# A two-layer decoder trunk: where the small loads stand, who sums the second adaLN part, the order ahead of the experts, and 2 MB pieces for units of four

## The chip, the core and the metric

The kernel runs on one core of one Trainium2 chip. The metric is the device time of one execution in microseconds. The engines named below are PE (TensorE matmuls), DVE (VectorE), ACT (ScalarE), POOL (GpSimd) and SP (SyncE, which here does nothing but issue loads). The 16 DMA engines of the core carry every transfer.

## The reference

256 tokens of width 1024 go through two layers. Each layer is conditioned on one vector `c`, whose product with `w_ada` gives six rows of 1024 (shift, scale and gate, once for the token mixing and once for the experts). The weights of the 32 experts of each layer are by far the most of the bytes.

```python
for l in range(DEPTH):                                   # DEPTH = 2
    mod = (silu(c) @ w_ada[l] + b_ada[l])[:, None, :]    # [1024] x [1024, 6144]
    sh1, sc1, gt1, sh2, sc2, gt2 = split(mod, 6)
    h = x * (1 + sc1) + sh1
    q, k, v, u, vs = split(h @ w_in[l], ...)             # five sections of 512 columns
    att = rms_norm(diff_attention(rope(q), rope(k), v, lam)) # 4 heads, 2 maps of 64
    sg  = chunk_spatial_gate(gelu(u), gelu(vs), ...)     # zu * (w_spatial @ LN(zv) + b)
    x = layer_norm(alpha * x + (1 + gt1) * (concat(att, sg) @ w_out[l]))
    h = x * (1 + sc2) + sh2
    ffn = hier_moe(h, ...)      # top 1 of 4 groups, then top 2 of its 8 experts
    x = layer_norm(alpha * x + (1 + gt2) * ffn)          # expert: (silu(h wg) * (h wu)) wd
```

## The kernel before

**One stream of weights.** `add_*` functions write down, in order, every weight piece of both layers (`stream`). A piece is 1 MB, and it goes into one of 18 slots of 1 MB (`RING`). `pump` (L174) issues pieces on SP as long as a slot is free, and `done` (L204), called where the last instruction that reads a piece is written down, gives its slot back. SP works strictly in order, and each load waits for the landing of the load eight before it on the queue. So the transfers run at most 18 pieces ahead of the engines, and a load whose slot is not free holds back all that stand behind it.

**Small loads.** Biases, norms, rotary tables, router weights and the like (`setup_loads`, L326, some thirty loads of 16 bytes to 256 KB) stand in a list `later`; `pump` issues three of them behind each piece, from the first piece on. The last of them are the router weights of both layers, in tiles `rst` of 128 x 384 numbers; POOL copies them into `wrs` (`reorder`, L354). The tile `four` of `scale_rows` (L387), a pattern of ones that PE uses to spread small rows, has the same tag (`aT`) as `rst`, so it takes the buffer of the first `rst`, and DVE writes it in the middle of the rotary step.

**The order of layer 0 up to the experts.** Sections Q, K, VS, U and V of `h @ w_in` on PE, rotary on DVE (`rope`, L679), transposes of q and k (`qk_T`), VS and U with their norm, then `spatial` and four heads of attention (`scores`, `a_T`, `att`). Four PSUM buffers of tag `s` serve the two products `mix` of `spatial` and the first scores; DVE frees the first two with `zu * mix` (L811). Then `wo` (the product with `w_out`, L924), `residual` (L959) and `normalise` (L582).

**Sums of `w_ada`.** The parts `s1` (shift and scale of the mixing), `s2` (those of the experts) and the gates `g1` and `g2` of `w_ada` are 8 MB, 8 MB, 4 MB and 4 MB per layer. `ada_fold` (L485) is a generator of DVE instructions: each multiplies a quarter of a 1 MB piece by a column of silu(c) and adds it to an accumulator that lies in the first piece, four per piece. `fold_on(n)` takes `n` more instructions of part `s2`, `fold_too(n)` of the next layer's `s1`. `ada_sum` (L429) sums the accumulator over the partitions on PE, and multiplies on PE what was not folded. In layer 0 DVE folds pieces 0 to 3 of `s2`; pieces 4 to 7 come behind `w_out`, and PE multiplies them in `routing`.

**Routing and experts.** `routing` (L983) transposes x, forms `h`, the logits, and the places of the tokens. It also splits x into three bf16 parts (`part` on ACT, `subtract` on PE) for the gather on PE. `gate_sum` forms the gate on PE, `gate_copy` copies it out of PSUM. The experts run in 11 units: units 0 to 5 hold two experts with 64 slots each, units 6 to 10 four experts with 32 slots each. For each unit come `gate`, `up` (`proj`, L1265) and `down` (`dps`). Each expert's matrix is 2 MB and is loaded as two pieces of 1 MB, all first halves of a unit ahead of the second halves. Places 0 to 3 hold fixed experts; which expert stands at a later place is read from the sorted choices of the tokens, and an expert that no token chose is passed over by its loads.

Of the kernel before, what the change touches and what calls it, by code (L numbers as in the profile page):

```python
# [27 lines left out]
def kernel(  # L28
# [89 lines left out]

    def down_parts(i):
        if i == NU - 1:  # L120
            return [((0, 4), (0, 512)), ((0, 2), (512, 1024)), ((2, 4), (512, 1024))]
        return [((0, 2), (0, 1024)), ((2, 4), (0, 1024))]

    def add_experts(l):
# [19 lines left out]
    for l in range(L):  # L144
# [22 lines left out]
    slots = [ring.tile([P, 4 * 512], F32, tag=f"w{i}", name=f"w{i}") for i in range(RING)]  # L167
    free = list(range(RING))
    held, slot_of, taken = {}, {}, {}
# [4 lines left out]
    def pump(limit=RING):  # L174
        while pos["issued"] < len(stream) and pos["issued"] - pos["done"] < limit:
            key, src = stream[pos["issued"]]
            slot_of[key] = free.pop(0)
# [13 lines left out]
            v = slots[slot_of[key]]  # L191
# [8 lines left out]
            for d, s_ in later[:3]:  # L200
                nc.sync.dma_start(d, s_)
            del later[:3]

    def done(*keys):  # L204
        for key in keys:
            held.pop(key)
            free.append(slot_of.pop(key))
# [35 lines left out]
    nc.sync.dma_start(badac, b_ada.rearrange("l (s p k) -> p l s k", s=6, k=KD))  # L243
# [374 lines left out]
    def mixing(l, fp, y_prev, sts):  # L618
# [30 lines left out]
        if l > 0:  # L649
# [255 lines left out]
        S.copy(vv[:, 1, :], section(l, V_, 1))  # L905
        ovs = [py.tile([P, 512], F32, tag="s", name=f"att{qc}").rearrange("t (h d) -> t h d", h=H) for qc in range(NTC)]
# [42 lines left out]
        for tci in range(NTC):
            for h in range(2):  # L950
                if tci == 0 and h == 0 and l + 1 < L:
                    asum = ada_sum(l + 1, "s1", 8)
                elif tci == 0 and h == 1 and l + 1 < L:
                    ada_cols(l + 1, 0, asum, fp)
                wo(tci, h, 0)
                residual(tci, h, o_ps[tci][h], gt1, fp)
            normalise(tci)
# [25 lines left out]
    def routing(l, wr, fp):  # L983
# [5 lines left out]
        def part(a, tci):  # L989
# [3 lines left out]
            for h in range(2):  # L993
                k = slice(4 * h, 4 * h + 4)
                S.copy(parts[:, a, tci, k], left[tci][h].rearrange("t (k d) -> t k d", k=4))

        def subtract(a, tci):
            if a == 0:
                left[tci] = [py.tile([P, 512], F32, tag="s", name=f"left{tci}{h}") for h in range(2)]
            for h in range(2):  # L1000
                k = slice(4 * h, 4 * h + 4)
                if a == 0:
                    T.matmul(left[tci][h], ident, X[:, tci, k, :], start=True, stop=False)
                T.matmul(left[tci][h], minus, parts[:, a, tci, k], start=False, stop=True, skip_group_check=(a > 0))
# [19 lines left out]
        if l == 0:  # L1024
            asum2 = ada_sum(l, "s2", KD // 2)
            ada_cols(l, 2, asum2, fp, py)
            gc, bc = affine_cols(l, 1)
            subtract(0, 0)
            make_hT(hk, gc, bc, 0, early)
            part(1, 0)  # L1030
        else:
            gc, bc = affine_cols(l, 1)
# [463 lines left out]
```

## Time and profile before

| what | us |
|---|---|
| median of 3 runs | 1222.11 |
| lowest and highest | 1221.09 and 1224.03 |
| the profiled execution | 1222.26 |
| its span | 1220.4 |
| PE busy, DVE busy, ACT busy | 1064.3, 356.2, 156.8 |

The profiled execution's time is 1.86 us over its span, which is what lies around it. 467.63 MB were moved in the span. The timelines give the start of an instruction from the beginning of the span, its duration, and in brackets how long the engine had been idle and what ended that.

### The profile page before, as it was taken

Reading aid. Unit: us, or ns where it says so; the run is one execution under the profiler, and the core shown is the slowest. Engines: PE = TensorE matmul, PEld = TensorE weight load, DVE = VectorE, ACT = ScalarE, POOL = GpSimd, SP = SyncE. Lnnn points to the kernel's source line nnn. Section 1 sums busy time; section 2 is a strip of 40 time slices with the busy share of each in tenths; the row PEclk is TensorE's granted clock in tenths of the full one; section 3 lists DMA queues with packets and bytes.
Section 4 is the critical chain, followed back from the end, with each engine's and each line's share of the span. In section 5 each row is a group of like instructions: output and inputs, shape, how many; then the busy total and the mean of one; then the engine's idle time right before and its main releaser. Section 6 shows DMA issues by size and latency. Waiting matters only on the chain. (4 is left out here: it accounts for less than half of the span.)

```text
span 1220.4 us, 14341 instructions
## 1 busy us (share of the span) xinstructions
PE 1064.3 (87%) x5353; PEld 425.6 (35%) x5353; DVE 356.2 (29%) x845; ACT 156.8 (13%) x384; POOL 24.2 (2%) x35
## 2 busy tenths in 40 slices
PE   6999998999997886788789998799999878677875
PEld 2465453434342221132135654343434222122221
DVE  1386767211120100030148535721212001003103
ACT  2033132101010100000022323210101000000000
POOL 0200000000000000000000400000000000000000
PEclk8999999999999888999999999999999989889888
DMA  9999988999999999999999954889999999999995
GB/s 320 363 405 368 418 308 357 379 405 421 421 420 421 421 420 422 422 420 420 393 398 398 400 178 140 335 337 404 421 420 421 422 421 422 421 421 421 420 409 193
DMA packets 92494, 467.63 MB, mean 383 GB/s; under 512 B 12445, under 2 KB 12977, under 8 KB 44546
## 3 DMA queue, kind: packets, MB, share of 16 engines
q1 hardware_dynamic: 92050, 465.86, 94.8%
q8 instruction: 45, 0.74, 0.2%
q10 hardware_dynamic: 288, 0.52, 0.1%
q0 software_dynamic: 80, 0.26, 0.1%
q14 instruction: 31, 0.25, 0.1%
HBM read 484.44 MB, written 1.05 MB: 398 GB/s over the span
## 5 line engine op out<-in xcount | busy, mean ns | idle before, releaser
L1270 PE MATMUL up<-w,XT_moe 128*32 128x512 f32 (+1 forms) x1024 | 196.3, 650 | 37.8 <-DMA w<-in_w_up_dram 37.7
L1360 PE MATMUL dps<-w,eaT_moe 128*32 128x512 f32 (+1 forms) x1024 | 196.2, 635 | 37.8 <-DMA w<-in_w_down_dram 29.2
L1270 PE MATMUL gate<-w,XT_moe 128*32 128x512 f32 (+1 forms) x1024 | 192.8, 656 | 27.3 <-DMA w<-in_w_gate_dram 25.1
L1270 PEld LDWEIGHTS up<-w,XT_moe 128*32 128x32 f32 (+1 forms) x1024 | 53.6, 128 | 170.1 <-issue 102.7
L1326 DVE TENSOR_TENSOR act_moe<-sg_moe,up 128x512 f32<-128x512 f32 x22 | 15.1, 687 | 327.5 <-PE up L1270 292.7
L1360 PEld LDWEIGHTS dps<-w,eaT_moe 128*32 128x32 f32 (+1 forms) x1024 | 52.7, 126 | 165.3 <-issue 98.1
L1270 PEld LDWEIGHTS gate<-w,XT_moe 128*32 128x32 f32 (+1 forms) x1024 | 53.1, 129 | 160.1 <-issue 108.0
L624 PE MATMUL sec<-w,hT_front 128*128 128x512 f32 x192 | 86.5, 605 | 2.6 <-DMA w<-in_w_in_dram 2.4
L1366 DVE TENSOR_TENSOR eo_moe<-dps,gt 128x512 f32<-128x512 f32 x44 | 30.4, 691 | 199.9 <-PE dps L1360 199.9
L1279 PE MATMUL y<-eo_moe,wt_moe 128*128 128x512 f32 x176 | 84.9, 607 | 1.6 <-DVE eo_moe L1366 1.6
L1249 PE MATMUL gps<-G_moe,Xp_moe 128*128 128x256 bf16 (+1 forms) x672 | 64.5, 250 | 3.7 <-DVE G_moe L1223 1.5
L1255 DVE TENSOR_SCALAR XT_moe<-gps,gc,bc 128x128 f32<-128x128 f32 x88 | 30.6, 404 | 123.8 <-PE gps L1249 123.8
L1316 ACT ACTIVATE sg_moe<-gate 128x512 f32<-128x512 f32 x22 | 13.1, 597 | 416.4 <-PE gate L1270 416.4
L1249 PEld LDWEIGHTS <-Xp_moe 128*128 128x128 bf16 x672 | 53.2, 98 | 21.9 <-issue 12.9
L624 PEld LDWEIGHTS sec<-w,hT_front 128*128 128x128 f32 x192 | 36.1, 193 | 45.7 <-issue 41.2
L494 DVE SCALAR_TENSOR_TENSOR w<-w,csl,w 128x512 f32<-128x512 f32 x68 | 47.3, 760 | 0.0
L1279 PEld LDWEIGHTS y<-eo_moe,wt_moe 128*128 128x128 f32 x176 | 30.2, 191 | 43.7 <-issue 40.3
L1294 ACT COPY wt_moe<-wtps 128x256 f32<-128x256 f32 x22 | 8.2, 372 | 286.8 <-PE wtps L1292 286.8
L1258 ACT ACTIVATE XT_moe<-gps,bc,gc 128x128 f32<-128x128 f32 x88 | 33.7, 456 | 41.2 <-PE gps L1249 41.2
L633 PE MATMUL sec<-w,hT_front 128*128 128x512 f32 x64 | 30.1, 625 | 1.9 <-DVE hT_front L647 1.9
L816 PE MATMUL u<-hT_front,w 128*128 128x256 f32 x128 | 28.8, 379 | 0.0
L929 PE MATMUL wo<-w,zu_front 128*128 128x512 f32 x64 | 28.1, 592 | 0.0
(282 smaller groups left out, 745.1 us busy)
## 6 DMA issues: line engine op xcount, KB each, us to landing
w<-in_w_gate_dram SPq DMA_DIRECT2D x128, 1024.0 KB, 17.3
w<-in_w_up_dram SPq DMA_DIRECT2D x128, 1024.0 KB, 17.5
w<-in_w_down_dram SPq DMA_DIRECT2D x120, 1024.0 KB, 16.0
w<-in_w_ada_dram SPq DMA_DIRECT2D x40, 1024.0 KB, 15.4
w<-in_w_in_dram SPq DMA_DIRECT2D x20, 1024.0 KB, 14.9
w<-in_w_ada_dram SPq DMA_DIRECT2D x16, 512.0 KB, 6.1
w<-in_w_out_dram SPq DMA_DIRECT2D x8, 1024.0 KB
w<-in_w_down_dram SPq DMA_DIRECT2D x16, 512.0 KB, 11.3
```

Of the source, the lines that this page charges most:

```text
L494: yield V.scalar_tensor_tensor(acc[:, c], w[:, c], csl[:, k:k + 1], acc[:, c], op0=ALU.mult, op1=ALU.add)
L624: T.matmul(ps, hT[:, k, tci * P:(tci + 1) * P], held["in", l, s, k // 4][:, k % 4, :], start=(k == 0), stop=(k == KD - 1))
L633: T.matmul(ps, hT[:, k, tci * P:(tci + 1) * P], held["in", 0, s, hf][:, k % 4, :], start=(k == 0), stop=(k == KD - 1))
L816: T.matmul(ps[:, 0:NT], held["in", l, U_, k // 4][:, k % 4, g * P:(g + 1) * P], hT[:, k, :], start=(k == 0), stop=(k == KD - 1))
L929: T.matmul(o_ps[tci][h], (cat, zu)[hf][:, kk, tci * P:(tci + 1) * P], w[:, kk, :], start=(hf == 1 and kk == 0), stop=(hf == 0 and kk == 3))
L1249: T.matmul(ps[:, k - kk].rearrange("p j s -> p (j s)"), parts[:, a, tci, k, :], g[:, tci, js[0] * P:(js[-1] + 1) * P], start=(a == 0 and t ...
L1255: V.tensor_scalar(dst, ps[:, k - kk, i, :], gc[:, k:k + 1], bc[:, k:k + 1], op0=ALU.mult, op1=ALU.add)
L1258: S.activation(dst, ps[:, k - kk, i, :], AF.Identity, scale=gc[:, k:k + 1], bias=bc[:, k:k + 1])
L1270: T.matmul(ps[c0:c0 + w], xt[:, k, c0:c0 + w], held[nm, l, place, k // 4][:, k % 4, :], start=(k == 0), stop=(k == KD - 1))
L1279: T.matmul(y[tci][h], wt[:, tci, :], eo[:, h, :], start=(i == 0), stop=(i == NU - 1))
L1360: T.matmul(dps[h][s0:s0 + w], aT[:, kk, s0:s0 + w], held["down", l, place, part][:, kk - ks[0], c0:c0 + 512], start=(kk == 0), stop=(kk == ...
L1366: V.tensor_tensor(eo[:, h, :], dps[h], gt2[:, h * 512:(h + 1) * 512], op=ALU.mult)
```

## The change

It has five parts.

1. **Small loads.** `pump` issues none of `later` behind the first eleven pieces; from the twelfth on three behind each. `badac` joins the list. The copies by POOL are written down after the first columns of the mixing.
2. **Part `s2` of layer 0.** Pieces 4 to 7 stand ahead of `w_out` in the stream, and `ada_fold` runs over all eight. `fold_on(12)`, which stood there without effect in layer 0, now takes pieces 4 to 6; piece 7 follows after section V. `ada_sum` and `ada_cols` move into `wo` in both layers.
3. **Routing.** Both layers take one order: the affine columns and the first half of `h` ahead of `normalise(1)`, first casts of both halves ahead of the second ones, and `gate_copy` directly behind the last cast. `left` of the second half lies in another pool.
4. **Layer 1's head.** Section Q is loaded ahead of the second half of `g1`, and the second half of `gate_sum` follows section Q.
5. **Units 6 to 9.** An expert's matrix is one load of 2 MB into two neighbouring slots (`choose`); all other pieces stay at 1 MB.

```diff
+    def in_parts(i):
+        return [(0, 8)] if (FIXED + WIDE) // 2 <= i < NU - 1 else [(0, 4), (4, 8)]
...
         if l > 0:
-            add_ada(l, "g1", range(4))
-            add_in(l, [Q_, K_, VS_])
+            add_ada(l, "g1", range(2))
+            add_in(l, [Q_])
+            add_ada(l, "g1", range(2, 4))
+            add_in(l, [K_, VS_])
...
             add_ada(l + 1, "s1", range(4, 8))
+            add_ada(l, "s2", range(4, 8))
         add_out(l)
-        if l == 0:
-            add_ada(l, "s2", range(4, 8))
...
+    both = [ring.tile([P, 8 * 512], F32, tag=f"w{i}", name=f"w{i}") for i in range(RING // 2)]
+    slots = [both[i // 2][:, i % 2 * 2048:i % 2 * 2048 + 2048] for i in range(RING)]
...
+    def choose(whole):
+        pairs = [i for i in free if i ^ 1 in free]
+        if whole:
+            return [min(pairs[0], pairs[0] ^ 1), max(pairs[0], pairs[0] ^ 1)] if pairs else None
+        if last and last[0] ^ 1 in free:
+            return [last[0] ^ 1]
+        return (pairs or free)[:1] or None
...
-            for d, s_ in later[:3]:
-                nc.sync.dma_start(d, s_)
-            del later[:3]
+            if pos["issued"] >= 12:
+                for d, s_ in later[:3]:
+                    nc.sync.dma_start(d, s_)
+                del later[:3]
...
-        for k in range(4 if (l, part) == (0, "s2") else KD):
+        for k in range(KD):
...
         S.copy(vv[:, 1, :], section(l, V_, 1))
+        if l == 0:
+            fold_on(6)
...
         part(0, 0)
-        if l == 0:
-            asum2 = ada_sum(l, "s2", KD // 2)
-            ada_cols(l, 2, asum2, fp, py)
...
+        gc, bc = affine_cols(l, 1)
+        make_hT(hk, gc, bc, 0, early, both=False)
+        gsum = gate_sum(l, "g2", 5)
+        subtract(0, 0)
+        normalise(1)
...
+        gate_sum(l, "g2", 5, gsum)
         subtract(1, 1)
         part(2, 1)
+        gr = gate_copy(l, 5, gsum, fp)
...
+            assert not later
+            for f in copies:
+                f()
```

**SP, start of layer 0, before.** The router weights (`rst0`, `rst1`) and their neighbours on the queue. `w10` to `w13` hold sections K and VS of `w_in`, `w14` to `w17` pieces 0 to 3 of `s2`, `w0` and `w1` section U.

```order
L201 DMA lncol_144<-in_ln2_b_dram 128x2x8
L201 DMA rst0_front0_179<-in_w_group_dram 128x32
L201 DMA rst0_front0_179<-in_w_router_dram 128x4x64
L197 DMA w12_90<-in_w_in_dram 128x4x512
L201 DMA rst1_front0_180<-in_w_group_dram 128x32
L201 DMA rst1_front0_180<-in_w_router_dram 128x4x64
L197 DMA w13_91<-in_w_in_dram 128x4x512
L197 DMA w14_92<-in_w_ada_dram 128x2048
```

**SP, the same loads after.** `w8` holds pieces 2 and 3 of `s2`, `w0` section U, each as two halves of a pair.

```order
L224 DMA w8_86<-in_w_ada_dram 128x2048
L229 DMA wsp0_front0_168<-in_w_spatial_dram 128x4x128
L229 DMA lncol_134<-in_ln1_g_dram 128x2x8
L229 DMA lncol_134<-in_ln1_b_dram 128x2x8
L224 DMA w0_78<-in_w_in_dram 128x4x512
L229 DMA lncol_134<-in_ln2_g_dram 128x2x8
L229 DMA lncol_134<-in_ln2_b_dram 128x2x8
L229 DMA rst0_front0_169<-in_w_group_dram 128x32
L224 DMA w0_78<-in_w_in_dram 128x4x512
L229 DMA rst0_front0_169<-in_w_router_dram 128x4x64
```

The router weights stood ahead of section VS and all of `s2`; now they stand behind these and behind section U.

**SP, after, later in layer 0.** Each row is a load, `x4` four in a row: the piece of `s1` that goes into the first half of `w8`, and pieces 4, 5 and 6 of `s2`, which all go into its second half; then piece 7 into `w0`, and `w_out`.

```order
L224 DMA w7_85<-in_w_ada_dram 128x2048
L224 DMA w8_86<-in_w_ada_dram 128x2048 x4
L224 DMA w0_78<-in_w_ada_dram 128x2048
L224 DMA w0_78<-in_w_out_dram 128x4x512
L224 DMA w1_79<-in_w_out_dram 128x4x512
```

Before, pieces 4 to 7 had four slots of their own, behind `w_out`; here three pieces share one half, one after the other.

**DVE, layer 0, before, from the norm of `zv` to the softmax.** `sgps` are the norm's scale and shift, `w2` the first piece of the next layer's `s1`, `lam` the attention's lambda, `zu<-zu,mix` the end of `spatial`, `mx` the first maximum over `scores`.

```order
L722 TENSOR_SCALAR zv_front0_361<-zv_front0_361,sgmv_488,sgrs_513 128x128 x8
L727 TENSOR_TENSOR zv_front0_361<-zv_front0_361,sgps_571 128x512 x2
L727 TENSOR_TENSOR zv_front0_361<-zv_front0_361,sgps_575 128x512 x2
L492 TENSOR_SCALAR w2_80<-w2_80,csl_171 128x512 x4
L385 COPY lam_170<-lamps_607 128x2
L811 TENSOR_TENSOR zu_front0_524<-zu_front0_524,mix_610 128x4x128
```

**DVE, the same place after.**

```order
L751 TENSOR_SCALAR zv_front0_352<-zv_front0_352,sgmv_479,sgrs_504 128x128 x8
L756 TENSOR_TENSOR zv_front0_352<-zv_front0_352,sgps_562 128x512 x2
L756 TENSOR_TENSOR zv_front0_352<-zv_front0_352,sgps_566 128x512 x2
L522 SCALAR_TENSOR_TENSOR w7_85<-w8_86,csl_161,w7_85 128x512 x12
L520 TENSOR_SCALAR w1_79<-w1_79,csl_161 128x512 x4
L413 COPY lam_160<-lamps_612 128x2
L840 TENSOR_TENSOR zu_front0_515<-zu_front0_515,mix_615 128x4x128
```

Twelve instructions have come in between, the sums of the pieces 4, 5 and 6 that SP's list above puts into one half slot.

**ACT, routing of layer 1, before.** `rsy` is the root of `normalise(1)`, `Xp` the bf16 parts, `hT` the transposed input of the router.

```order
L558 ACTIVATE rsy_4603<-rsv_4601 128x1
L559 ACTIVATE rsy_4603<-rsy_4603 128x1
L991 CAST Xp_moe1_4615<-X_98 128x8x128
L615 ACTIVATE hT0_moe1_4616<-hTps_4619,bc1_1_4631,gc1_1_4630 128x128 x4
L615 ACTIVATE hT1_moe1_4617<-hTps_4624,bc1_1_4631,gc1_1_4630 128x128 x4
L995 CAST Xp_moe1_4615<-left00_4644 128x4x128
```

**ACT, the same place after.**

```order
L1025 CAST Xp_moe1_4542<-X_89 128x8x128
L643 ACTIVATE hT0_moe1_4543<-hTps_4546,bc1_1_4558,gc1_1_4557 128x128 x4
L643 ACTIVATE hT1_moe1_4544<-hTps_4551,bc1_1_4558,gc1_1_4557 128x128 x4
L586 ACTIVATE rsy_4598<-rsv_4596 128x1
L587 ACTIVATE rsy_4598<-rsy_4598 128x1
L643 ACTIVATE hT1_moe1_4544<-hTps_4611,bc1_1_4558,gc1_1_4557 128x128 x4
```

The first cast and the first half of `hT` have moved ahead of the root of `normalise(1)`.

## Rows read from the trace of the kernel before

**Rows 1.** The page: transfer rate in 40 slices of 30.5 us each.

```profile
GB/s 320 363 405 368 418 308 357 379 405 421 421 420 421 421 420 422 422 420 420 393 398 398 400 178 140 335 337 404 421 420 421 422 421 422 421 421 421 420 409 193
```

**Rows 2.** Stretches: busy PE, PEld, DVE, ACT, POOL, clock, DMA share, GB/s.

```profile
210.00:220.00 10.00, 10.00 (x42) 3.39 (x41) 3.82 (x5) 0.00 (x0) 0.00 (x0) 0.86 0.52 198
...
720.00:750.00 30.00, 26.36 (x82) 12.41 (x78) 15.56 (x35) 2.99 (x8) 0.00 (x0) 0.98 0.52 175
840.00:1140.00 300.00, 257.31 (x1370) 88.05 (x1366) 42.89 (x80) 17.92 (x44) 0.00 (x0) 0.93 1.01 421
```

**Rows 3.** Timeline of PE, layer 0: start, duration, instruction, [idle before, releaser].

```profile
156.90 1.04 PE L603 MATMUL hTps<-ident,X 128*128 128x128 f32 x8
157.87 1.06 PE L433 MATMUL ada_s<-w,onec 128*32 128x512 f32 x8
158.75 3.62 PE L438 MATMUL ada_s<-w,csl 128*32 128x512 f32 x32
163.07 1.09 PE L478 MATMUL adaT<-ident,adar_moe 128*64 128x128 f32 x8 [0.71 <-ACT adar_moe L473]
...
185.41 4.94 PE L1270 MATMUL gate<-w,XT_moe 128*64 128x512 f32 x22 [0.76 <-ACT gr_moe L520]
```

**Rows 4.** Timeline of DVE, layer 0.

```profile
56.12 0.64 DVE L391 COPY four_front<-ident 16x128 f32<-16x128 f32 x1
56.89 0.69 DVE L685 TENSOR_TENSOR ropea_front<-sec,cos 128x512 f32<-128x512 f32 x1
...
60.76 0.69 DVE L685 TENSOR_TENSOR ropea_front<-sec,cos 128x512 f32<-128x512 f32 x1 [1.85 <-PE sec L633]
...
62.37 0.41 DVE L690 TENSOR_TENSOR ropea_front<-ropea_front,ropeb_front 128x256 f32<-128x256 f32 x1
...
73.10 5.39 DVE L494 SCALAR_TENSOR_TENSOR w<-w,csl,w 128x512 f32<-128x512 f32 x8
...
93.22 0.16 DVE L385 COPY lam<-lamps 128x2 f32<-128x2 f32 x1 [0.67 <-PE lamps L384]
94.50 0.69 DVE L811 TENSOR_TENSOR zu_front<-zu_front,mix 128x512 f32<-128x512 f32 x1 [1.12 <-PE mix L808]
```

**Rows 5.** Timelines of SP and POOL, layer 0: router weights loaded, and copied.

```profile
40.62 0.60 SPq L201 DMA_DIRECT2D rst_front<-in_w_router_dram  x1
...
46.27 0.40 POOL L356 COPY wr<-rst_front 128x256 f32<-128x256 f32 x1
```

**Rows 6.** Stretches, columns as above: the start, and one of 2 KB rows.

```profile
0.00:60.00 60.00, 47.42 (x164) 20.16 (x165) 14.33 (x40) 10.03 (x15) 10.36 (x25) 0.94 0.99 341
60.00:70.00 10.00, 9.76 (x29) 4.51 (x28) 9.08 (x18) 2.36 (x3) 0.00 (x0) 1.00 1.03 400
...
660.00:670.00 10.00, 10.00 (x34) 5.84 (x33) 8.46 (x25) 3.09 (x5) 0.00 (x0) 1.00 1.05 385
```

**Rows 7.** DMA issues: count, KB of one, median us from issue to landing.

```profile
out_dram<-o_moe ACTq DMA_DIRECT2D x2, 256.0 KB, 2.2
```

**Rows 8.** Timelines of PE, DVE and ACT, routing of layer 1.

```profile
742.75 1.04 PE L603 MATMUL hTps<-ident,X 128*128 128x128 f32 x8
...
748.19 0.39 PE L1004 MATMUL left<-Xp_moe,minus 128*128 128x512 bf16 x1 [3.54 <-ACT Xp_moe L991]
...
768.53 3.65 PE L1270 MATMUL gate<-w,XT_moe 128*64 128x512 f32 x16 [1.37 <-ACT gr_moe L520]
...
745.01 1.28 DVE L586 BATCH_NORM_STATS2 bnst<-X 128x6 f32<-128x512 f32 x2
...
748.60 0.17 DVE L546 TENSOR_SCALAR gc<-modc 128x8 f32<-128x8 f32 x1
...
749.34 2.90 ACT L615 ACTIVATE hT_moe<-hTps,bc,gc 128x128 f32<-128x128 f32 x8 [1.21 <-DVE gc L550]
```

**Rows 9.** Timeline of PE, start of layer 1.

```profile
621.06 8.80 PE L624 MATMUL sec<-w,hT_front 128*128 128x512 f32 x16 [2.39 <-DMA w<-in_w_in_dram]
...
630.90 7.10 PE L624 MATMUL sec<-w,hT_front 128*128 128x512 f32 x16 [0.16 <-DVE hT_front L613]
```

More of the change, by code (lines that the diff above doesn't have):

```diff
@@ L176, in pump @@
             key, src = stream[pos["issued"]]
-            slot_of[key] = free.pop(0)
+            whole = key[0] in ("gate", "up", "down") and key[3] in ((0, 8), ((0, 4), (0, 1024)))
+            got = choose(whole)
+            if got is None:
+                break
+            for i in got:
+                free.remove(i)
+            slot_of[key] = got
+            last[:] = got[-1:]
             cond = {}
@@ L190, in pump @@
                 src = src(taken[l, place][1] if place >= FIXED else None)
-            v = slots[slot_of[key]]
+            v = both[got[0] // 2] if whole else slots[got[0]]
             if len(src.shape) == 4:
@@ L206, in done @@
             held.pop(key)
-            free.append(slot_of.pop(key))
+            free.extend(slot_of.pop(key))
             pos["done"] += 1
@@ L954, in mixing @@
                     ada_cols(l + 1, 0, asum, fp)
+                elif tci == 1 and h == 0:
+                    asum2 = ada_sum(l, "s2", KD)
+                elif tci == 1 and h == 1:
+                    ada_cols(l, 2, asum2, fp)
                 wo(tci, h, 0)
                 residual(tci, h, o_ps[tci][h], gt1, fp)
-            normalise(tci)
+                if tci == 0 and h == 0:
+                    fold_on(4)
+            if tci == 0:
+                normalise(0)
     def residual(tci, h, ps, gt, pool):
@@ L1156, in routing @@
         hTs.clear()
-        return gc, bc, Xp, posm, rest, places, gsum
+        return gc, bc, Xp, posm, rest, places, gr
     def spill(l, gc, bc, Xp, ovc, ci, gt, mp):
@@ L1210, in last_rows, with experts @@
         return fg, fb
-    def experts(l, gc, bc, Xp, posm, rest, places, gsum, mp):
+    def experts(l, gc, bc, Xp, posm, rest, places, gr, mp):
         Gs, Ws, XTs = {}, {}, {}
@@ L1268, in proj @@
             for k in range(KD):
+                part = next(q for q in in_parts(i) if q[0] <= k < q[1])
                 for place, c0, w in UNITS[i]:
                     T.matmul(ps[c0:c0 + w], xt[:, k, c0:c0 + w],
-                             held[nm, l, place, k // 4][:, k % 4, :], start=(k == 0), stop=(k == KD - 1))
-                if k % 4 == 3:
-                    done(*[(nm, l, place, k // 4) for place, _, _ in UNITS[i]])
+                             held[nm, l, place, part][:, k - part[0], :], start=(k == 0), stop=(k == KD - 1))
+                if k == part[1] - 1:
+                    done(*[(nm, l, place, part) for place, _, _ in UNITS[i]])
             return ps
@@ L1396 @@
             pump()
-            for f in copies:
-                f()
             def x_in():
@@ L1427 @@
         mp = moe_pool(l)
-        gc, bc, Xp, posm, rest, places, gsum = routing(l, wrs[l], mp)
-        y, sts, fin = experts(l, gc, bc, Xp, posm, rest, places, gsum, mp)
+        gc, bc, Xp, posm, rest, places, gr = routing(l, wrs[l], mp)
+        y, sts, fin = experts(l, gc, bc, Xp, posm, rest, places, gr, mp)
         if l + 1 == L:
```

64 lines of the change are left out of this document (24 added, 40 removed).

## The prediction

> **What bounds the kernel now.** I read the rates over the span first, then single stretches, and then the order of the instructions where the transfers stop. For most of the span the DMA engines move 420 to 422 GB/s [rows 1], and in units of four experts they are busy all the time while PE is not: 257.31 of 300 us, DMA share 1.01 [rows 2]. There only the transfers count. But the rate falls in two places, ahead of the experts of each layer: 198 at 210 us, 175 between 720 and 750 us [rows 2]. PE is busy there nearly without a gap. The ring of 18 pieces is full and nothing is loaded until an engine gives a slot back. So a microsecond on the chain PE, DVE, ACT ahead of the experts is a microsecond of the total, in either layer, and a lost stretch of transfers is never made up behind it, since the transfers are at their rate there. That is the frame of the sum: layer 0's chain, layer 1's chain, and the rate in units 6 to 9.
>
> **Small loads (layer 0).** They go from places behind the first pieces to places behind the twelfth and later ones. The last are the router weights. In the trace SP issues those of layer 0 by 41.2 us and POOL has copied them at 46.67 us [rows 5], well ahead of their reader. But `four` lies in the same buffer as the first `rst`, so DVE must wait with it for POOL's copy; it ran at 56.12 us without any wait [rows 4]. After the change 21 pieces' worth of weights and x, 22.0 million bytes, and some 0.7 million of small loads (by their shapes) are ahead of `rst`. The stretch to 60 us moved 341 GB/s, thus 20.5 million bytes, the next one goes at 400 [rows 6]; the remaining 2.2 million take 5.6 us, and the load lands near 66.5. Copies of 0.6 us and `four` of 0.64 follow, so the rotation of k starts near 68.0 in place of 56.89. Behind `four` on DVE stand both rotations of k, all folds, and the norm of `zv`; on PE, the transposes of k and behind them sections VS and U. The two rotations ended at 62.8 after 5.9 us, of which 1.85 were a wait for PE that is now over [rows 4]; they end at 68.0 + 4.0 = 72.0. **A = +9.2 us.** Bounds: were everything ahead moved at 421 from the start, `rst` would land near 58 and A be about +1; if the wait inside stays, +11. I take the value from the row whose bytes are the same.
>
> **Pieces 4 to 6 of `s2` (layer 0).** They pass, one after the other, through one half slot: SP may issue piece 5 only when DVE has folded piece 4, and piece 6 only when it has folded piece 5. Piece 4 is long there, since it waits only for the fold of piece 3. The twelve folds stand on DVE ahead of `lam` and of `zu * mix`. One fold takes 5.39 / 8 = 0.674 us [rows 4], twelve take 8.1. Between them lie two loads of 1 MB on a queue that SP's wait has emptied. A store of 256 KB lands 2.2 us after its issue [rows 7]; 0.62 of that is its transfer at 421 GB/s, so 1.6 is fixed, and 1 MB takes 2.5 + 1.6 = 4.1. Two are 8.2. Two waits of DVE for PE, 0.67 and 1.12 [rows 4], disappear. **B = 8.1 + 8.2 - 1.8 = +14.5 us**, between 12 (a shorter latency) and 18 (transfers still queued ahead). Nothing covers it: the second pair of scores needs the PSUM buffers that `zu * mix` frees, PE stands there with section V behind them, and SP itself holds back piece 7, `w_out` and the experts. Piece 7's four folds, 2.7 us, come after section V, where DVE has waits; nothing is added for them.
>
> PE stands idle for about ten microseconds in each of the two waits. After a wait of 2.39 us its sixteen matmuls of a section took 8.80 us, the same sixteen without a wait 7.10 [rows 9]: **+1.7**, counted once; 0 to 3.4.
>
> **Routing of layer 0.** From the end of `wo` at 156.90 to the first expert matmul at 185.41 are 28.5 us [rows 3]. `ada_sum` takes 1.06 + 3.62 there and `adaT` 0.71 + 1.09. The multiplications of 3.62 go altogether; the rest, 1.06 and 1.09, goes into `wo`, where PE is busy, and costs 2.1 there. With layer 1's new order (next) 21.5 remain. **-28.5 + 21.5 + 2.1 = -4.9 us**; -2 to -7.
>
> **Routing of layer 1.** From 742.75 to 768.53 are 25.8 us [rows 8]. The first half of `hT` on ACT waits for `gc`, which DVE writes behind `normalise(1)`: 748.60 [rows 8]. Without `normalise(1)`, which begins at 745.01 [rows 8], `gc` is made there, and `hT` starts 4 us sooner; PE's wait of 3.54 us goes. Then `normalise(1)` is late: its 3.6 us of DVE now stand behind, and the second half of `h` comes only 3 us sooner. The gate's copy, for which PE waited 1.37 us, now stands ahead of the gather. Together -3.0 - 1.2 = -4.2. At the head Q's load saves the 2.39 us of its wait, but part of the gate's sum comes behind Q: -1.3 of a possible -2.4 [rows 9]. **-5.5 us**; -3 to -7.
>
> **2 MB pieces.** Units 6 to 9 of both layers are 201 million bytes, 478 us at 421. An SBUF row of a piece becomes 16 KB in place of 8. In a stretch of 2 KB rows (`w_in`) the rate is 385 [rows 6], of 8 KB rows 421. 16 x 8192 bytes take 340 and 311 ns, so each of three more starts of a row costs 9.7 ns. One start less per 16 KB gives 613 in place of 622.6 ns, 428 GB/s, and 7.5 us on the whole. **-6 us**, as experts without tokens are passed over; 0 to -7.5, zero if the rows are cut at 8 KB. A unit waits longer for its first matmul, since a pair must be there whole, but five of the nine pairs, 25 us of transfers, are queued behind the four in use, and a pass over them takes 7 us.
>
> **Sum.** 9.2 + 14.5 + 1.7 - 4.9 - 5.5 - 6 = +9.0 on 1222.26, the profiled execution's own time (span 1220.4 and 1.86 around it; 0.15 above the median): **1231 us**.
>
> **Rivals.** *The router weights land early* (A near +1, no idle PE there): 1223. For it: small loads are what slows the start, and the first 13 MB lose them. Against: they only move, ahead of `rst` still. *The transfers, not the engines, end layer 0's front*, the case on the other side: then A, B and the gain of that routing are all absorbed, and -5.5 - 6 gives 1211. It decides if DMA's share ahead of the experts stays near 1. For it: 363 to 418 GB/s in slices two to five, up to 152 us [rows 1]. Against: 0.52 at 210 us [rows 2], where PE is fully busy. *The 2 MB pieces bring nothing*, because rows are cut or a pair is waited for: 1237. The Trainium skill, "DMA: Bandwidth & Descriptors", "Rules for kernel authors", asks for 1 MiB or more per DMA for the full bandwidth; every piece has that already, so by that rule the sum is 1237 too. *PE falls back to 1.2 GHz between its bursts in units of four* and becomes their bound: 257 us at a clock of 0.93 would be 479 for 300 [rows 2], far over 1300. The Trainium skill, "TensorE: Matmul & The Clock Gate", "HAM oscillation", tells of kernels that wait for DMA between matmuls and lose the clock so. Against: at 0.93 the units' present waits already cost almost nothing.
>
> **Chances.** Forecast 0.54, early router weights 0.13, absorbed 0.14, nothing from 2 MB 0.17, clock 0.02. The range 1216 to 1242 holds the forecast with its bounds, the first and the third rival; the absorbed case, the clock and the ends of the bounds stay out. About 0.2% is what a measurement of this kernel can tell from no change. Below 1219.7 lie the absorbed case and a tail of the first: 0.18. Within 0.2%: 0.10. Above: 0.72.
>
> **What would show it.** A: `four` near 67 us behind POOL. B: DVE waiting twice for a load of `w_ada`, about 4 us each, ahead of `zu * mix` near 118 to 120, and PE idle there. Layer 1: first expert matmul 21 to 22 us behind the end of `wo`. 2 MB: near 428 GB/s in units of four. It is wrong if DVE does not stand at those two loads, or if the first experts of layer 0 start before 195 us (forecast: near 206).

## The result: slower by 2.7%, and where the time went

| | us |
|---|---|
| before, median of 4 runs beside the changed kernel | 1223.07 |
| changed, median of 4 runs | 1257.66 (1254.87 to 1259.13) |
| ratio, 95% interval | 1.0269 (1.0239 to 1.0298) |
| the profiled execution and its span | 1259.13, 1257.5 |
| forecast | 1231 (1216 to 1242) |

The sign was right, the size was not: +34.6 us in place of +9.0. The same events, read from both traces (their spans lie 37.1 us apart, the medians 34.6), show where the distance between the two kernels grows:

| event | before | changed | shift | forecast |
|---|---|---|---|---|
| layer 0: second rotation of k ends | 62.78 | 77.47 | +14.7 | +9.2 |
| `zu * mix` starts | 94.50 | 130.62 | +36.1 | +23.7 |
| end of `wo` (first `hTps`) | 156.90 | 197.06 | +40.2 | +27.5 |
| first expert matmul | 185.41 | 223.74 | +38.3 | +20.5 |
| layer 1: second Q section | 630.90 | 670.32 | +39.4 | +16.2 |
| end of `wo` | 742.75 | 782.11 | +39.4 | +16.2 |
| first expert matmul | 768.53 | 810.47 | +41.9 | +12.0 |
| end of the span | 1220.4 | 1257.5 | +37.1 | +9.0 |

Nearly all of it is lost in layer 0 before `zu * mix`. The page of the changed kernel says the same in its rate over 40 slices (answers [rows 1]) and in the granted clock of TensorE below it: slices four and five, 94 to 157 us, fall from 368 and 418 to 265 and 149 GB/s, and the clock digits of slices three to five read 7, 8 and 8.

```profile
GB/s 347 303 382 265 149 409 280 330 378 410 420 425 341 428 429 426 429 428 376 416 392 405 395 362 160 163 343 404 422 421 426 430 426 429 427 428 428 420 412 211
PEclk8978898999999788778999999799999988788998
```

**Layer 0's front.** DVE's timeline in the changed kernel (answers [rows 4]; start, duration, instruction, [idle before, releaser]): `four` waits 16.44 us for POOL, which itself waits for a load of the router weights (first row, from POOL's timeline), and each fold of pieces 4, 5 and 6 waits for its load.

```profile
72.09 0.40 POOL L384 COPY wr<-rst_front 128x256 f32<-128x256 f32 x1 [2.55 <-DMA rst_front<-in_w_router_dram]
...
72.52 0.21 DVE L419 COPY four_front<-ident 16x128 f32<-16x128 f32 x1 [16.44 <-POOL wr L384]
...
110.92 2.74 DVE L522 SCALAR_TENSOR_TENSOR w<-w,csl,w 128x512 f32<-128x512 f32 x4 [3.34 <-DMA w<-in_w_ada_dram]
118.62 2.74 DVE L522 SCALAR_TENSOR_TENSOR w<-w,csl,w 128x512 f32<-128x512 f32 x4 [4.96 <-DMA w<-in_w_ada_dram]
126.31 2.74 DVE L522 SCALAR_TENSOR_TENSOR w<-w,csl,w 128x512 f32<-128x512 f32 x4 [4.95 <-DMA w<-in_w_ada_dram]
...
130.62 1.28 DVE L840 TENSOR_TENSOR zu_front<-zu_front,mix 128x512 f32<-128x512 f32 x2
```

PE follows, with one wait for each of the two, and computes at the low clock behind both: section VS, 16 matmuls, takes 9.11 us, the next section 7.03, and the first scores behind the second wait 1.39 in place of 0.49.

```profile
74.86 1.09 PE L726 MATMUL qkTps<-ident,ropea_front 128*128 128x128 f32 x4 [13.74 <-DVE ropea_front L719]
79.58 9.11 PE L652 MATMUL sec<-w,hT_front 128*128 128x512 f32 x16
...
88.96 7.03 PE L652 MATMUL sec<-w,hT_front 128*128 128x512 f32 x16
...
113.24 0.49 PE L767 MATMUL s<-qk_front 64*128 64x128 f32 x4
...
131.36 1.39 PE L767 MATMUL s<-qk_front 64*128 64x128 f32 x4 [16.56 <-DVE zu_front L840]
```

Stretches of the changed kernel (columns as in [rows 2]) show what that leaves of the transfers. From 60 to 107 us the queue never empties. Then pieces 5 and 6 go through the half slot one after the other, each issued when the fold ahead of it has ended (at 113.69 and 121.39 us), and the second piece of `w_out` waits for one more fold (issued at 139.42). These stretches run at 27 to 289 GB/s, and the granted clock of PE falls to 0.50, which is 1.2 GHz.

```profile
0.00:60.00 60.00, 47.79 (x164) 20.31 (x165) 11.70 (x34) 10.05 (x15) 2.63 (x18) 0.91 0.93 327
60.00:107.00 47.00, 33.26 (x104) 19.42 (x103) 30.47 (x77) 11.12 (x16) 7.59 (x7) 0.82 1.02 387
...
110.00:120.00 10.00, 4.64 (x35) 3.51 (x34) 4.12 (x7) 1.67 (x2) 0.00 (x0) 0.89 0.30 106
120.00:130.00 10.00, 0.00 (x0) 0.00 (x0) 5.05 (x10) 0.00 (x0) 0.00 (x0) 0.50 0.76 289
130.00:140.00 10.00, 8.64 (x21) 4.38 (x22) 8.76 (x26) 3.44 (x16) 0.00 (x0) 0.59 0.07 27
```

**The routing.** From the end of `wo` to the first expert matmul are 26.7 us in layer 0 (28.5 before) and 28.4 in layer 1 (25.8 before, [rows 8]). The timeline of layer 1's routing, ACT, DVE and PE: the eight copies of `hT(0)` stand on ACT ahead of `rsy` of `normalise(1)`, DVE waits 2.19 us for it and PE 2.47 for the normalised X. Behind that wait both products of the logits take 3.61 us.

```profile
785.24 2.89 ACT L643 ACTIVATE hT_moe<-hTps,bc,gc 128x128 f32<-128x128 f32 x8
...
787.99 0.23 ACT L586 ACTIVATE rsy<-rsv 128x1 f32<-128x1 f32 x1
...
788.49 0.22 DVE L592 SCALAR_TENSOR_TENSOR rst<-rsy,rsv 128x1 f32<-128x1 f32 x1 [2.19 <-ACT rsy L587]
...
790.00 1.88 PE L631 MATMUL hTps<-ident,X 128*128 128x128 f32 x8 [2.47 <-DVE X L616]
...
791.74 3.61 PE L1053 MATMUL rt<-wr,hT_moe 128*128 128x36 f32 x16
...
795.22 3.61 PE L1053 MATMUL rt<-wr,hT_moe 128*128 128x36 f32 x16
```

**Units of four.** Two stretches of the kernel before, in the units of four of either layer; then three of the changed kernel: the end of layer 0's units of two, and the units of four of either layer. 428 and 426 GB/s stand where 421 stood, as forecast; but in layer 0 the queue is empty for 3.4 us just ahead of them.

```profile
370.00:560.00 190.00, 148.08 (x854) 44.40 (x847) 25.51 (x46) 7.90 (x19) 0.00 (x0) 0.90 1.01 421
985.00:1160.00 175.00, 137.16 (x738) 41.31 (x742) 22.89 (x38) 8.70 (x20) 0.00 (x0) 0.87 1.01 421
...
380.00:390.00 10.00, 10.00 (x48) 4.01 (x47) 1.98 (x5) 1.50 (x4) 0.00 (x0) 1.00 0.44 161
390.00:560.00 170.00, 122.55 (x671) 35.40 (x673) 14.23 (x28) 6.29 (x15) 0.00 (x0) 0.81 1.01 428
1030.00:1200.00 170.00, 124.16 (x726) 39.52 (x726) 22.18 (x37) 8.16 (x20) 0.00 (x0) 0.84 1.01 426
```

### The profile page after: what moved, and what is told of

Its sections match the earlier page's. It is cut to its first block, busy times and chain, and to the rows that moved or that the text cites. A ratio compares the mean times of both kernels' runs of the same rounds, so it can differ in the third digit from the quotient of the medians.

```text
span 1257.5 us, 13892 instructions
## 1 busy us (share of the span) xinstructions
PE 1057.6 (84%) x5319; PEld 431.9 (34%) x5321; DVE 366.9 (29%) x857; ACT 158.2 (13%) x388; POOL 24.1 (2%) x35
## 5 line engine op out<-in xcount | busy, mean ns | idle before, releaser
L1296 PE MATMUL up<-w,XT_moe 128*32 128x512 f32 (+1 forms) x1024 | 188.6, 651 | 42.0 <-DMA w<-in_w_up_dram 42.0
L1296 PE MATMUL gate<-w,XT_moe 128*32 128x512 f32 (+1 forms) x1024 | 184.1, 650 | 31.7 <-DMA w<-in_w_gate_dram 31.7
L522 DVE SCALAR_TENSOR_TENSOR w<-w,csl,w 128x512 f32<-128x512 f32 x72 | 50.0, 762 | 13.3 <-DMA w<-in_w_ada_dram 13.2
L1305 PEld LDWEIGHTS y<-eo_moe,wt_moe 128*128 128x128 f32 x176 | 30.2, 191 | 43.6 <-issue 40.2
L960 PE MATMUL wo<-w,cg_front 128*128 128x512 f32 x64 | 28.9, 597 | 0.0
```

The lines of the kernel that those rows point to most:

```text
L522: yield V.scalar_tensor_tensor(acc[:, c], w[:, c], csl[:, k:k + 1], acc[:, c], op0=ALU.mult, op1=ALU.add)
L960: T.matmul(o_ps[tci][h], (cat, zu)[hf][:, kk, tci * P:(tci + 1) * P], w[:, kk, :], start=(hf == 1 and kk == 0), stop=(hf == 0 and kk == 3))
L1296: T.matmul(ps[c0:c0 + w], xt[:, k, c0:c0 + w], held[nm, l, place, part][:, k - part[0], :], start=(k == 0), stop=(k == KD - 1))
L1305: T.matmul(y[tci][h], wt[:, tci, :], eo[:, h, :], start=(i == 0), stop=(i == NU - 1))
```

## The experiments

Ratios are to runs of the kernel before on the same chip; comparisons across the table go by them. 0.1% is 1.2 us.

| kernel | median us | ratio (95%) |
|---|---|---|
| changed | 1257.66 | 1.0269 (1.0239 to 1.0298) |
| `e1_four_alone` | 1256.41 | 1.0281 (1.0261 to 1.0300) |
| `e2_pe_half` | 1236.76 | 1.0123 (1.0102 to 1.0143) |
| `e3_both` = e1 + e2 | 1220.93 | 0.9973 (0.9955 to 0.9991) |
| `e4_one_mb` | 1254.80 | 1.0279 (1.0254 to 1.0304) |
| `e5_old_routing` = e3, routing as before | 1217.97 | 0.9966 (0.9954 to 0.9978) |
| `e6_norm_first` = e3, `normalise(1)` first | 1208.36 | 0.9884 (0.9865 to 0.9903) |
| `e7_before_2mb` | 1218.63 | 0.9976 (0.9966 to 0.9986) |
| `e8_before_head` | 1219.64 | 0.9977 (0.9967 to 0.9986) |
| `e9_norm_only` | 1243.66 | 1.0166 (1.0138 to 1.0194) |
| `e10_pieces_early` | 1212.49 | 0.9916 (0.9893 to 0.9938) |
| `e11_old_loads` = e6, small loads as before | 1205.78 | 0.9863 (0.9840 to 0.9887) |
| `e12_one_mb` = e6, 1 MB | 1214.41 | 0.9927 (0.9907 to 0.9948) |

### Layer 0's front: one wait behind another

**`e1_four_alone`** takes away what made `four` wait.

```diff
-    def scale_rows(fp):
+    def scale_rows(zv):
...
-        four = fp.tile([NROW, 4, 32], F32, tag="aT", name="four")
+        four = zv[0:NROW, 1, 0:P].rearrange("r (a b) -> r a b", a=4)
...
-            scale_rows(fp)
+            scale_rows(zv)
```

> The changed kernel with one edit: `four` is written into the part of `zv` that is still unused, no longer into the buffer that the router weights' `rst` held. The router weights arrive as late as before the edit. Theory: the late buffer holds DVE up by 14 to 17 us, so `four` runs near 58 us in place of 72.5 (when the last row of `rw` has landed), the second rotation of k ends near 64, `zu * mix` starts near 116 in place of 130.6, and the time is 1241 to 1244. Rival (the transfers end layer 0's front, so what DVE gains is waited for later): `four` runs early too, but the end of `wo` stays near 197 and the time near 1257.

The rival was right. `four` ran at 56.09 us, the second rotation ended at 63.25, and nothing was gained: 1.0281 beside 1.0269. DVE's timeline in this kernel, and two stretches of it, say why: it reached piece 4 at 93.3 us, 14 us sooner than in the changed kernel, and then stood 16.59 us there. The fold of piece 4 starts near 110 in both, although SP had issued its load by 90.2 us here and by 97.8 in the changed kernel: what was queued ahead of the load set its arrival, not the time at which the half slot came free. PE did nothing from 100 to 120.

```profile
56.09 0.21 DVE L419 COPY zv_front<-ident 16x128 f32<-16x128 f32 x1
...
109.90 2.74 DVE L522 SCALAR_TENSOR_TENSOR w<-w,csl,w 128x512 f32<-128x512 f32 x4 [16.59 <-DMA w<-in_w_ada_dram]
...
100.00:110.00 10.00, 0.00 (x0) 0.00 (x0) 0.10 (x1) 0.00 (x0) 0.00 (x0) 0.56 0.69 289
110.00:120.00 10.00, 0.00 (x0) 0.00 (x0) 4.84 (x8) 0.00 (x0) 0.00 (x0) 0.50 0.30 105
```

**`e2_pe_half`** leaves the lock on `four` and gives pieces 4 to 7 back to PE; **`e3_both`** has both edits.

```diff
+        add_out(l)
+        if l == 0:
             add_ada(l, "s2", range(4, 8))
-        add_out(l)
...
     def ada_fold(l, part):
         acc = held["ada", l, part, 0][:, 0, :]
-        for k in range(KD):
+        for k in range(4 if (l, part) == (0, "s2") else KD):
...
-                    asum2 = ada_sum(l, "s2", KD)
+                    asum2 = ada_sum(l, "s2", KD if l else KD // 2)
```

> The changed kernel with one edit: pieces 4 to 7 of layer 0's `s2` are loaded behind `w_out` and multiplied by PE in `ada_sum` (which stays where the change put it, in `wo`), not folded by DVE. Theory: the three waits of DVE of 3.3, 5.0 and 5.0 us and the folds between them go, `zu * mix` starts 19 us sooner (near 111.5); PE multiplies 3.6 us more in `wo`; the time is 1240 to 1243. If only the folds cost and the waits move elsewhere: 1249. If transfers end the front: 1257.

> Both edits, `four` in `zv` and pieces 4 to 7 multiplied by PE. Theory: the two losses lie one behind the other on DVE and add, so 1257.7 - 15 - 16 = 1227 (1224 to 1230). Rival: both hide the same wait (the transfers of the front), so the second edit brings less than 8 us beside the first and the time is 1234 or more.

`e2_pe_half` started `zu * mix` at 110.72 and came out at 1236.76, some 18 to 21 us below the changed kernel, a little more than expected. `e3_both` started it at 96.58 (94.50 before) and came out at 1220.93, lower than expected. In both (first `e2_pe_half`, then `e3_both`) DVE waits there for PE as before, and for no load:

```profile
110.72 0.69 DVE L841 TENSOR_TENSOR zu_front<-zu_front,mix 128x512 f32<-128x512 f32 x1 [1.12 <-PE mix L838]
...
96.58 0.69 DVE L841 TENSOR_TENSOR zu_front<-zu_front,mix 128x512 f32<-128x512 f32 x1 [1.12 <-PE mix L838]
```

On the same chip the lock on `four` is thus worth 1236.76 - 1220.93 = 15.8 us where the pieces are out of the way and nothing where they are not; the pieces are worth 1256.41 - 1220.93 = 35.5 us where `four` is out of the way. The two losses do not add, because the second is a wait until a fixed time (the arrival of piece 4) and swallows the first.

**`e10_pieces_early`** asks what makes piece 4 late: the bytes queued ahead of it, or the one half slot. DVE folds all eight pieces, as in the change, but they stand eight places sooner in the stream (with `four` in `zv` and `normalise(1)` first, as in `e6_norm_first` below).

```diff
         if l + 1 < L:
+            add_ada(l, "s2", range(4, 8))
             add_ada(l, "g1", range(4))
             add_ada(l + 1, "s1", range(4, 8))
-            add_ada(l, "s2", range(4, 8))
         add_out(l)
```

> `four` in `zv`, `normalise(1)` ahead of `hT(0)`, and DVE folds all eight pieces of layer 0's `s2` as in the change; but pieces 4 to 7 are loaded ahead of `g1` and of the second four of layer 1's `s1`, eight places sooner in the stream. Theory (the long wait is for bytes that are queued ahead of piece 4): it lands near 88 us, before DVE comes to it, the folds run without waiting, `zu * mix` comes 8 us later than with PE's multiplications (near 104 instead of 95.7), `wo` is 3.6 us shorter: 1211 to 1214. Rival (the half slot through which the pieces pass is the cause, whatever their place): DVE still waits about 5 us twice and the time is above 1220.

1212.49, as the theory had it. DVE's timeline: the twelve folds run as one block of 8.02 us behind the norm of `zv`, without any wait, and `zu * mix` follows at 103.00.

```profile
91.01 2.46 DVE L756 TENSOR_TENSOR zv_front<-zv_front,sgps 128x512 f32<-128x512 f32 x4
93.40 8.02 DVE L522 SCALAR_TENSOR_TENSOR w<-w,csl,w 128x512 f32<-128x512 f32 x12
101.35 1.65 DVE L520 TENSOR_SCALAR w<-w,csl 128x512 f32<-128x512 f32 x4
103.00 1.26 DVE L840 TENSOR_TENSOR zu_front<-zu_front,mix 128x512 f32<-128x512 f32 x2
```

So the place in the stream was the fault, not the folding by DVE. At the new place each piece also has a slot of its own, or the folds could not run without a load between them; so this run takes the bytes ahead of piece 4 and the shared half slot away together. That the bytes made piece 4 late is seen in `e1_four_alone`; the waits of 5 us for pieces 5 and 6 are the half slot's. The folding may still cost more than PE's multiplications do (0.9916 beside 0.9884 of `e6_norm_first`, with intervals that just overlap; in the traces the first expert starts at 189.85 and 183.71 us).

### The routing: one item of ACT's queue

**`e5_old_routing`** puts the routing of before back into `e3_both`; **`e6_norm_first`** keeps the new order there and moves one call; **`e9_norm_only`** moves that call in the changed kernel and leaves all else.

```diff
         part(0, 0)
         gc, bc = affine_cols(l, 1)
+        normalise(1)
         make_hT(hk, gc, bc, 0, early, both=False)
         gsum = gate_sum(l, "g2", 5)
         subtract(0, 0)
-        normalise(1)
```

> The kernel with both edits (`four` in `zv`, pieces 4 to 7 multiplied by PE) and, beside them, the routing in the order of before for both layers: `normalise(1)` back in `mixing`, the second `hTps` on the other PSUM pool, the gate's copy behind the first gather; `ada_sum` stays in `wo`. The prediction held that the new order saves 4.2 us in layer 1 and about 0.5 in layer 0, so going back would cost: 1225 to 1226. The theory from the traces (the new order makes PE wait 2.5 us for `X` ahead of the second `hTps` and compute the logits at 1.2 GHz; routing 26.7 us in either layer against 25.8 in layer 1 before and 28.5 - 6.5 = 22.0 in layer 0): going back saves 0.8 + 4.7, so 1215 to 1216.

> The kernel with both edits and one more: in the routing, `normalise(1)` stands ahead of the copies of `hT(0)`, so that ACT makes `rsy` before those eight copies. Theory: DVE's 2.2 us wait for `rsy` and PE's 2.5 us wait for `X` go, in both layers: -4.4, and up to 1.5 us a layer more if PE then keeps 2.4 GHz through the logits: 1213 to 1217. Rival (the logits are what ends the routing, at 1.2 GHz whatever stands ahead): the routing keeps 26.7 us, 1220 to 1222.

> The changed kernel with one edit alone: `normalise(1)` ahead of the copies of `hT(0)` in the routing. The two losses of layer 0's front stay. Theory (each routing falls to 20.0 us at a full clock, as with both other edits): 26.7 to 20 in layer 0 and 28.4 to 20 in layer 1, so -15 and 1241 to 1244. Rival (in the run with both other edits something else of the front brought part of it): 1250.

`e5_old_routing` does not differ from `e3_both` (0.9966 and 0.9973). The new order as it was written brought nothing; but the second expectation overstated it too, since without `ada_sum` the old order took 26.8 us in layer 0, not 22.0. Moving `ada_sum` into `wo`, with PE multiplying pieces 4 to 7, put 5.8 us there (1.06 + 3.62 + 1.09 by [rows 3]) and took only 1.7 out of that routing (28.5 to 26.8); no run makes this move alone.

`e6_norm_first` gained 0.89%, about 11 us, more than either expectation. The same stretch, end of `wo` to the first expert, takes 20.0 us in both layers. Rows of the two routings in `e3_both` (first two) and in `e6_norm_first` (last two):

```profile
164.49:191.18 26.69, 23.30 (x155) 15.18 (x153) 12.20 (x45) 12.18 (x28) 0.00 (x0) 0.81 0.67 268
745.00:771.68 26.68, 23.28 (x155) 15.37 (x153) 12.21 (x45) 12.19 (x28) 0.00 (x0) 0.81 0.47 178
...
163.67:183.71 20.04, 18.34 (x155) 11.59 (x153) 12.21 (x45) 12.16 (x28) 0.00 (x0) 1.00 0.89 359
737.20:757.25 20.05, 18.33 (x154) 11.57 (x152) 12.22 (x45) 12.16 (x28) 0.00 (x0) 1.00 0.65 236
```

DVE and ACT do the same 12.2 us of work; PE's busy time falls from 23.3 to 18.3, since the granted clock is 1.00 and not 0.81. The timeline of layer 1 in `e6_norm_first` shows the cause: `rsy` stands ahead of the copies, PE waits 0.79 us in place of 2.47, and each product of the logits takes 1.95 us in place of 3.61.

```profile
741.43 0.20 ACT L587 ACTIVATE rsy<-rsv 128x1 f32<-128x1 f32 x1 [1.00 <-DVE rsv L585]
...
743.41 1.09 PE L632 MATMUL hTps<-ident,X 128*128 128x128 f32 x8 [0.79 <-DVE X L617]
...
744.37 1.95 PE L1054 MATMUL rt<-wr,hT_moe 128*128 128x36 f32 x16
...
746.18 1.95 PE L1054 MATMUL rt<-wr,hT_moe 128*128 128x36 f32 x16
```

Of the 6.65 us of a routing, some 1.7 are the shorter wait; 5 are the clock. `e9_norm_only` gained 1.0% (14 us between the medians) with both routings at 20.04 us and a clock of 1.00: this gain, unlike that of `four`, does not depend on the rest, as transfers do not end the routing.

### 2 MB pieces

**`e4_one_mb`** is the changed kernel with `in_parts` always in halves, **`e12_one_mb`** the same in `e6_norm_first`, **`e7_before_2mb`** the kernel before with 2 MB pieces alone.

```diff
     def in_parts(i):
-        return [(0, 8)] if (FIXED + WIDE) // 2 <= i < NU - 1 else [(0, 4), (4, 8)]
+        return [(0, 4), (4, 8)]
```

> The changed kernel with units of four in 1 MB pieces as before the change, all else as changed. Theory from the two traces: layer 0 lost 5.6 us in its units (3.5 us of them an empty queue ahead of the first 2 MB load), layer 1 gained 4.8; so the time is within 2 us of 1257.7, and the stretch at units 5 to 6 of layer 0 shows no gap. The prediction's term for 2 MB: +6, so 1264. If layer 0's loss has another cause (its late start), 1262.

> The kernel before with one part of the change: 2 MB pieces in units 6 to 9, nothing else. The prediction's term: -6, so 1217. From the traces: -4.7 in layer 1; in layer 0 between 0 and +5, since the first 2 MB load of a layer has to wait for a pair, so 1219 to 1223. If the first 2 MB load does not stall from this start (pairs fall otherwise): 1215.

> The same kernel (`four` in `zv`, pieces 4 to 7 on PE, `normalise(1)` first) with units of four in 1 MB pieces. The prediction's term says +6: 1214. From the traces: +4.5 in layer 1, 0 to +1 in layer 0: 1212 to 1214. If the gain is only what the stall ahead of the first 2 MB load gives back: 1208.

In the changed kernel 2 MB made no difference (1.0269 with, 1.0279 without). From the kernel before they are worth 0.24% (2.9 us, interval 1.7 to 4.2), and in the last kernel 0.43% (5 us; the medians differ by 6.1). The traces show a gain in layer 1: from its first expert to DVE's last instruction are 448.6 us before and 444.5 in `e7_before_2mb`, 450.0 in `e4_one_mb` and 443.8 in the changed kernel. Between `e12_one_mb` and `e6_norm_first` it is only 448.7 and 446.6; but the traced run of `e12_one_mb` is its fastest, 4.8 us below its median, so this trace cannot say where the 5 us lie.

Layer 0 is another matter. In the changed kernel, in `e1_four_alone` and in `e9_norm_only`, whose experts start at 216 to 224 us, the queue stands empty for 2.1 to 3.4 us near 380, ahead of the first 2 MB load; in the kernels whose experts start at 183 to 205 us it does not. Nor does it in `e4_one_mb`, which starts them at 220 us with 1 MB pieces: its layer 0 takes 426.3 us from the first expert to the last, like the kernel before (426.4), where the changed kernel takes 431.9. So 2 MB pieces behind a late front lost in layer 0 what they gained in layer 1. Without the stall layer 0 takes 425 to 427 us with 2 MB, hardly less than with 1 MB; why it gains less than layer 1 stays open. Whether the pair of slots or a ring that was already full held that load up was not tried.

### Layer 1's head and the small loads

**`e8_before_head`** makes part 4 alone in the kernel before; **`e11_old_loads`** undoes part 1 in `e6_norm_first` (`later` from the first piece on, `badac` behind x, POOL's copies ahead of the first columns).

```diff
-            add_ada(l, "g1", range(4))
-            add_in(l, [Q_, K_, VS_])
+            add_ada(l, "g1", range(2))
+            add_in(l, [Q_])
+            add_ada(l, "g1", range(2, 4))
+            add_in(l, [K_, VS_])
...
             make_hT(lambda k: hT[:, k], gc, bc, 0, early)
-            gate_sum(l, "g1", 2, gsum1)
+            V.bn_stats(sts[1][:, 1, :], y_prev[1][1])
             normalise_psum(1, y_prev[1], sts[1])
             q0 = section(l, Q_, 0)
+            make_hT(lambda k: hT[:, k], gc, bc, 1, early)
+            gate_sum(l, "g1", 2, gsum1)
...
```

> The kernel before with one part of the change: in layer 1 Q's load stands ahead of the second half of `g1`, and the gate's second half is summed behind Q. The prediction's term -1.3: 1222. From the traces (from the last expert to the second Q section 4.5 us shorter): 1219. If the transfers set layer 1's front anyway: 1223.5.

> The kernel of `four` in `zv`, pieces 4 to 7 on PE and `normalise(1)` first, with part 1 of the change undone: the small loads stand behind the first pieces again, as before. Theory (the small loads cost SP the same issue time wherever they stand, and the second rotation of k ended at 62.8 before and at 63.3 here): within 2 us of 1208.4. Rival (the change's place for them lets the first weights come sooner): 1211 or more.

`e8_before_head`: 0.23%, 2.8 us faster (1.7 to 4.0), between the two expectations. Its trace has layer 1's first Q section 4.4 us closer to layer 0's first expert, but the routing of layer 1 took 27.3 us there (25.8 before).

`e11_old_loads`: 0.9863 beside 0.9884, with intervals that overlap. Part 1 brought nothing that can be seen; if anything it cost 2 to 3 us. SP is held near these loads at either place. In the changed kernel (SP's queue: start, duration until the next could be issued) the two rotary tables hold SP for 3.36 and 7.96 us between weight pieces of 0.4, and the router weights follow at 62 to 67. In `e11_old_loads` the same tables hold it for 2.85 and 0.47 us, and the 1 MB of `w_in` just ahead of them for 4.85.

```profile
27.18 3.36 SPq L229 DMA_DIRECT2D cos<-in_rope_cos_dram  x1
30.58 1.31 SPq L229 DMA_DIRECT2D badac<-in_b_ada_dram  x1
31.93 7.96 SPq L229 DMA_DIRECT2D sin<-in_rope_sin_dram  x1
...
62.40 2.21 SPq L229 DMA_DIRECT2D rst_front<-in_w_group_dram  x1
...
65.59 0.37 SPq L229 DMA_DIRECT2D rst_front<-in_w_router_dram  x1
...
67.05 0.60 SPq L229 DMA_DIRECT2D rst_front<-in_w_router_dram  x1
```

`e11_old_loads` is faster than both kernels of this study, by 1.4% (1.1 to 1.6) against the one before. It keeps of the change the routing with `normalise(1)` first, the head of layer 1, the 2 MB pieces and `ada_sum` in `wo`; `four` lies in `zv`, and PE multiplies pieces 4 to 7.

## Why the prediction fell short, step by step

**A, the router weights.** Mechanism right, size wrong, and place in the sum wrong. `four` did stand behind POOL's copy, at 72.5 us in place of 67; the rotations ended +14.7 where +9.2 was said. The load was taken to land at 66.5 from bytes alone, at 341 and then 400 GB/s (its sum as written gives 65.6, and its lower bound 54 and not 58; neither decides anything). The rows give 327 GB/s to 60 us and 304 from 60 to 70, with the queue busy all the while; SP issues the load that POOL waits for only at 65.59, and POOL copies it at 72.09. Three small loads behind every piece hold SP, and they are themselves ahead of `rst`. By itself A is 15.8 us (`e2_pe_half` to `e3_both`). In the changed kernel it is nothing (`e1_four_alone`).

**B, pieces 4 to 6.** This is the step that failed first, and by the experiments the dearest. "Piece 4 is long there, since it waits only for the fold of piece 3" looked at the slot alone. Piece 4 is the 35th MB of the stream; with x and the small loads 38.5 million bytes come ahead of its end. By the rates of [rows 6], 20.5 million to 60 us and 400 GB/s from there, it lands at 105, and DVE, 9.2 us later than the 90.9 of before, comes to it at 100 (102 with the 1.7 of the clock). The sum was one multiplication away, and it was made for `rst` but not here. In the trace 327 and 387 GB/s bring 37.8 million bytes by 107, and the fold starts at 110.92. The two loads behind it were seen rightly as waits of DVE; they cost 4.96 and 4.95 us, not 4.1. B by itself is 35.5 us (`e1_four_alone` to `e3_both`), 16.6 of them the wait for piece 4. The rival "the transfers end layer 0's front" was written down with the opposite sign: it was to absorb A and B; in truth the transfers up to piece 4 absorbed A and made B.

**The clock.** Said: +1.7, counted once. Section VS lost 2.1 us behind the first wait; from `zu * mix` to the end of `wo` 4.0 more were lost, of which 2.1 are the sums moved into `wo`, as forecast, and 1.9 the clock (the first section V took 9.00 us, not 7.09). The price itself was read at one place, 8.80 us behind a wait of 2.39 [rows 9]; in `e7_before_2mb` the same section takes 7.10 behind a wait of 2.38. So a wait of that length does not cost the clock every time.

**Routing.** Said: 21.5 us would remain in layer 0 and 4.2 be saved in layer 1. A routing that short can be had, though with another order: `e6_norm_first`, with `normalise(1)` first, shows 20.0. This is the second step that failed: "`normalise(1)` is late" followed DVE and not ACT, where its `rsy` now stood behind eight copies of 0.36 us; PE's wait of 3.54 us [rows 8] became one of 2.47 at another place, ahead of the logits, and the shorter wait was the dearer one: the routing of layer 1 ran at a granted clock of 0.93 behind the first and of 0.76 behind the second. Off by +5 in layer 0 and +7 in layer 1.

**Head.** Said -1.3; in the trace the second Q section comes 4.5 us closer to the last expert, and alone the edit measures 2.8. The whole wait of 2.39 us [rows 9] went, and with it the slower matmuls behind it (7.13 us in place of 8.80). From the last expert to the second Q section are 19.1 us before, 17.4 in `e7_before_2mb`, where the wait cost no clock, and 14.6 in the changed kernel.

**2 MB.** Said 428 GB/s and -6. The rate was right (428 and 426), and -6 is about what the times of `e12_one_mb` show; in the changed kernel layer 1 gained 4.8 us and layer 0 lost 5.6, of which 3.4 are a queue that ran empty ahead of the first pair. The sum had put nothing for that. The rule of the Trainium skill that was weighed, "DMA: Bandwidth & Descriptors", "Rules for kernel authors" (1 MiB or more per DMA), would have had no gain from 2 MB; the rows have 1.7% more rate. What the Trainium skill says in "TensorE: Matmul & The Clock Gate", "HAM oscillation", agrees in part: the clock in units of four fell from 0.90 and 0.87 to 0.81 and 0.84 as PE's longest waits grew from 2.1 to 3.9 us, but with PE busy 122.55 of 170 us the transfers stayed the bound. The 0.93 of [rows 2] is for a stretch that is nearly half units of two.

By the table of events, the two spans lie 28.1 us further apart than forecast: 12.7 of it in layer 0's front (A, B and the clock), 5.1 and 6.7 in the two routings, 6.8 in the units of four; the head gave 3.2 back. Of the 12.7, 5.5 are A's and 6.9 B's with the slow section VS. So no single term explains the miss: the front and the two routings weigh about the same.

## What to carry to other kernels

Before a load is given a new reader, count the bytes ahead of it in the stream and divide by the rate of the trace; a reader that comes sooner than that waits, whatever slot is free. Waits for a fixed arrival time do not add to delays ahead of them, so price two delays on one chain together, and undo them together, since undoing the earlier alone shows nothing. When an instruction is moved on one engine, follow the steps of it that run on the others: here two 0.2 us activations behind eight copies cost 6.7 us a layer.

## What the hardware showed beyond expectation

- The clock, not the wait, was most of the price of a short stop: behind 2.5 us of waiting ahead of the logits the routing ran at a granted clock of 0.76 to 0.86 and took 25.0 to 28.4 us, in both layers of five kernels; with a wait of 0.8 us it took 20.04 to 20.06 at 1.00, in both layers of five others. The length of the wait alone does not decide: 3.54 us at an earlier place [rows 8] left 0.93.
- The issue of a small load can hold SP far longer than that of a large one: 7.96 us for `sin`, a table of 32 KB, between pieces of 1 MB that take 0.4. In `e11_old_loads` the same load took 0.47, at another place in the queue, and there a piece of 1 MB took 4.85. What decides it was not tried.
- 1 MB asked for on an empty queue could be read 4.95 and 4.96 us after the fold that freed its slot had ended (5.16 and 5.00 in `e1_four_alone`), of which 2.5 are the transfer at 421 GB/s.
